# Values of all four recurrent heads in one projection of 512 columns, behind the gates of two heads

## The chip, the cores and the metric

The kernel runs on one core of one Trainium2 chip. The metric is the device time of one execution in microseconds, as the median of several runs. The engines named here are TensorE (PE; its weight loads are shown as PEld), VectorE (DVE), ScalarE (ACT), GpSimd (POOL) and SyncE (SP, which issues most DMAs). All products are made in float32 precision: an operand is split into a rounded high part and a remainder, and three matmuls (high by high, high by low, low by high) replace one.

## The reference, cut to what matters

Two blocks of two layers each run over 512 tokens of width 1024. The first block is an attention mixer, which the change leaves alone. Each layer of the second block has a recurrent mixer with eight heads of width 128 and then a gated FFN. The recurrent mixer is what the change touches:

```python
proj = h @ w_in                       # 512 x 1024 by 1024 x 4096
rq, rk, rv, rg, hq, hf, hi, hg = split(proj)      # 512 columns each: 4 heads of 128
r_out = retention_chunkwise(rotary(rq), rotary(rk) * 128 ** -0.5, rv, log_gamma)
q_h = silu(hq); k_in = (1 - lb) * sigmoid(-hf); log_f = log_sigmoid(hf) + log1p(lb * exp(-hf))
g_out = hgrn2_chunkwise(q_h, log_f, k_in, hi)
merged = concat(head_norm(r_out) * silu(rg), head_norm(g_out) * silu(hg))
x = x + g1 * (merged @ w_out)
```

The values are `hi` for the four HGRN2 heads and `rv` for the four retention heads. They are used as the right operand of the last product of a head, with the tokens on the partitions.

## The kernel before, in words

Activations lie with the 1024 features on the partitions, as eight pairs of tiles `hh`, `hl` (high part and remainder) of 128 x 512 tokens. A weight tile `wr` holds 128 x 1024 numbers (512 KB). One queue of weights serves the whole program: `next_w` gives the next one, starts the DMA of one some places ahead on SP's queue, and has ScalarE (L149) and VectorE (L150) split one into `wh` and `wl`. There are 2 buffers of `wr` and 3 of `wh` and `wl`. The array of host weights `w_in_2` is stored in the order in which `next_w` asks for it.

A gemm (`gemm`, `mm3`, L172 to L174) has a weight as stationary operand and 512 tokens as moving columns: 24 matmuls of 512 columns give one 128 x 512 tile `g` in PSUM with features on the partitions. Values are needed the other way round, with tokens on the partitions. `gemm_tok` (`tok_step`, L195 to L197) does that: the activations are stationary, 128 tokens at a time, and the weight is moving. A pair of heads has 256 value columns, so each matmul has 256 columns, and one PSUM tile `g` takes two blocks of tokens. `v_pair` makes the values of two heads: two weight tiles, two PSUM tiles, 96 matmuls, and two ScalarE copies (L1386) into the tile `v`, of which there are two buffers.

`ssm_layer` runs a layer. For each HGRN2 head it asks for the gate gemm (`hgrn_prep`: L1447 to L1458 give `k` and the cumulated logs `c`), the query gemm (`silu_ps`: three ScalarE steps L1463 to L1465, one VectorE step L1466), for every second head `v_pair`, and then the head itself (`hgrn`). A head is a chain of levels: VectorE and ScalarE make a tile `xl`, TensorE multiplies it with itself, and VectorE puts the result into the score tile `st`. The first level is L1532, then come L1537, L1546, six times L1558, and L1565; the product with the values is L1575. Normalising the output and turning it (`tail`, L1404) is left to the next head. The two gemms of head 0 are made in the stage before (`cross`), as `first`. After the HGRN2 heads follow four retention heads: two gemms with a rotation and a split each (`rotary`, `parts`, L217 and L218), for every second head `v_pair`, then score products, a decay mask (L1435) and the product with the values (L1440). Behind them come the eight output gates. In the first of the two layers VectorE also does background work, a matrix-vector product for the next modulation (L481).

The order on an engine is set by a scheduler when the program is built. Each engine then serves its own instructions in that order; where several are ready, the one that stands earlier in the program goes first. In the second block there are four PSUM buffers of tag `g`, four of tag `m` (products of the heads), 9 buffers of `u` (128 x 512 work tiles, also `k`, `c`, `q` of a head) and 3 of `xl`; a tile waits until a buffer of its tag is free.

The lines of `ssm_layer` that set the order are

```python
            q = silu_ps(oq)
            if h % 2 == 0:
                v = v_pair()
            tail = hgrn(l, h, k, c, q, [v[:, j, (h % 2) * P:(h % 2 + 1) * P] for j in range(4)], y[4 + h])
```

Of the kernel before, what the change touches and what calls it, by code (L numbers as in the profile page):

```python
# [20 lines left out]
P = 128  # L21
D = 1024
KT = 8
# [13 lines left out]
def tile_model(ctx: ExitStack, tc: tile.TileContext, a: dict, out: bass.AP, dbg=None):  # L37
# [1342 lines left out]

    def v_pair():
        os_ = [pt("g"), pt("g")]
        gemm_tok([(os_[0], hs2[0], 0), (os_[1], hs2[0], 2)])
        v = sb("v", [P, 4, 2 * P], F32, 2, sub[0])
        for i in range(2):
            act(v[:, 2 * i:2 * i + 2].rearrange("p a b -> p (a b)"), os_[i], AF.Copy)  # L1386
        return v
# [190 lines left out]
    def ssm_layer(l, hs, first):  # L1578
# [9 lines left out]
        tail = lambda: None  # L1588
        for h in range(HEADS):
            if h == 0:  # L1590
                (w, o), (w, oq) = first
            else:
                w = next_w()
                o = pt("g")
                gemm(o, w, hs)
            tail()
            k, c = hgrn_prep(l, h, o)
            if h > 0:
                w = next_w()
                oq = pt("g")  # L1600
                gemm(oq, w, hs)
            q = silu_ps(oq)
            if h % 2 == 0:
                v = v_pair()
            tail = hgrn(l, h, k, c, q, [v[:, j, (h % 2) * P:(h % 2 + 1) * P] for j in range(4)], y[4 + h])
        for h in range(HEADS):
            w = next_w()
            o = pt("g")
            gemm(o, w, hs)
            tail()  # L1610
            q = rotary(o, 1.0)
            q = (q, *parts(q))
            background(4)
            w = next_w()
            o = pt("g")
            gemm(o, w, hs)
            k = rotary(o, 128.0 ** -0.5)
            k = (k, *parts(k))
            if h % 2 == 0:
                v = v_pair()  # L1620
            tail = retention(h, q, k, [v[:, j, (h % 2) * P:(h % 2 + 1) * P] for j in range(4)], y[h])
        open_sub(f"mo{l}")
# [128 lines left out]
def _mixed(w, order):  # L1751
    w = np.asarray(w).reshape(KT, P, -1, P)
    r = []
    for t in order:
        if isinstance(t, tuple):
            b = w[:, :, list(t[:2])].reshape(2, 4, P, 2 * P).transpose(0, 2, 1, 3)
# [6 lines left out]
def _layout(i):  # L1763
# [22 lines left out]
    r["w_in_2"] = _f(np.stack([_mixed(g["w_in_2"][l], [  # L1786
        20, 16, (24, 25), 21, 17, 22, 18, (26, 27), 23, 19, 0, 4, (8, 9), 1, 5, 2, 6, (10, 11), 3, 7,
        12, 13, 14, 15, 28, 29, 30, 31]) for l in range(2)]))
# [77 lines left out]
```

## Time and profile before

| what | value |
|---|---|
| median of 3 runs | 2091.86 us (2086.92 to 2094.16) |
| time of the profiled execution | 2093.33 us |
| its span | 2091.5 us |
| TensorE busy | 2017.1 us, 96% of the span |
| TensorE weight loads busy | 1744.2 us, 83% |
| VectorE busy | 1416.8 us, 68% |
| ScalarE busy | 951.7 us, 46% |
| mean granted TensorE clock | 0.991 of full speed |

The span goes from the first to the last instruction of the profiled execution; its time is 1.8 us longer. Times below are in microseconds from the start of the span. A matmul is shown with its own duration, which overlaps that of the next one; the distance between two starts is what it costs in a stream. "x8" behind a row means that eight of the same kind were merged into it. A bracket at the end of a row gives the idle time of the engine before it and what ended it. The recurrent mixer of the first layer lies at about 766 to 998 us and that of the second at about 1436 to 1660 us.

### The profile page before, as it was taken

What the parts mean: (1) busy time and instruction counts of PE and PEld (TensorE: products, weight loads), DVE (VectorE), ACT (ScalarE), POOL (GpSimd) and SP (SyncE); (2) the same over time, 40 slices, a digit from 0 to 9 for tenths busy, and PEclk for the clock granted to TensorE, in tenths of its full rate; (3) what the DMA queues carried; (4) which work ended last, traced back from release to release, by engine and by line L of the source; (5) the groups of instructions that cost most, each with busy time, mean ns of one, the idle gap of its engine ahead of it and who ended that gap; (6) DMA issues with size and microseconds to landing.
All of it is one profiled execution on the core that took longest, in us unless ns stands there. A gap on an engine that the chain in (4) does not pass through costs nothing.

```text
span 2091.5 us, 30721 instructions
## 1 busy us (share of the span) xinstructions
PE 2017.1 (96%) x11642; PEld 1744.2 (83%) x11642; DVE 1416.8 (68%) x2733; ACT 951.7 (46%) x1655; POOL 204.0 (10%) x204
## 2 busy tenths in 40 slices
PE   5899999999999999999999999999999999999998
PEld 3798988899898889988888888888998888888887
DVE  6889998578667488888677775238876655444323
ACT  4536567343547456435453333226543544333322
POOL 5401011130101120000110000002000030000000
PEclk9999999999999999999999999999999999999999
DMA  7342224644011332255456664323122223232332
GB/s 266 100 134 85 93 92 132 213 138 133 31 61 51 121 125 81 84 169 184 146 159 215 217 209 144 101 83 101 60 71 72 90 73 108 94 101 92 92 103 76
DMA packets 96132, 245.97 MB, mean 118 GB/s; under 512 B 12592, under 2 KB 17952, under 8 KB 95728
## 3 DMA queue, kind: packets, MB, share of 16 engines
q1 hardware_dynamic: 94752, 242.90, 36.7%
q8 instruction: 92, 1.51, 0.3%
q0 software_dynamic: 656, 0.57, 0.1%
q10 hardware_dynamic: 576, 0.52, 0.1%
q14 instruction: 56, 0.46, 0.1%
HBM read 239.76 MB, written 4.19 MB: 117 GB/s over the span
## 4 chain that ended last, share of the span: by engine, by line
PE 79%; DVE 11%; ACT 3%; issue 2%; DMA 2%; POOL 1%; DVEq 0%; SPq 0%; POOLq 0%; ACTq 0%
PE g L173 19%; PE g L172 19%; PE g L174 19%; PE g L196 3%; PE g L197 3%; PE g L195 3%; PE m L1558 2%; PE m L947 2%; DVE gs L481 1%; DMA gr<-w_mod 1%; PE s L921 1%; DVE wl L150 1%; PE s L922 1%; PE m L940 1%; PE m L1575 1%
## 5 line engine op out<-in xcount | busy, mean ns | idle before, releaser
L173 PE MATMUL g<-hl,wh 128*128 128x512 f32 (+1 forms) x1320 | 508.2, 385 | 12.9 <-DVE hl L296 11.4
L174 PE MATMUL g<-hh,wl 128*128 128x512 f32 (+1 forms) x1320 | 504.9, 383 | 1.0 <-POOL wl L334 0.8
L172 PE MATMUL g<-hh,wh 128*128 128x512 f32 (+1 forms) x1320 | 505.2, 383 | 0.2 <-ACT wh L153 0.2
L150 DVE TENSOR_TENSOR wl<-wr,wh 128x1024 fp32r<-128x1024 f32 (+1 forms) x270 | 326.1, 1209 | 251.0 <-ACT wh L149 247.3
L149 ACT ACTIVATE wh<-wr 128x1024 fp32r<-128x1024 f32 (+1 forms) x270 | 281.9, 1044 | 411.6 <-PE g L173 369.1
L173 PEld LDWEIGHTS g<-hl,wh 128*128 128x128 f32 x1320 | 249.9, 189 | 62.2 <-DVE hl L296 17.7
L174 PEld LDWEIGHTS g<-hh,wl 128*128 128x128 f32 x1320 | 250.1, 189 | 45.5 <-POOL wl L334 1.1
L172 PEld LDWEIGHTS g<-hh,wh 128*128 128x128 f32 x1320 | 249.9, 189 | 44.2 <-ACT hh L292 0.7
L481 DVE SCALAR_TENSOR_TENSOR gs<-gr,cb 128x512 bf16<-128x512 f32 x304 | 209.9, 691 | 101.7 <-DMA gr<-ada_w 81.9
L197 PE MATMUL g<-wh,hl 128*128 128x256 f32 x704 | 202.3, 288 | 5.2 <-DVE hl L254 3.2
L196 PE MATMUL g<-wl,hh 128*128 128x256 f32 x704 | 203.8, 290 | 2.8 <-DVE wl L150 2.3
L195 PE MATMUL g<-wh,hh 128*128 128x256 f32 x704 | 203.5, 289 | 1.6 <-ACT hh L251 1.6
L235 POOL TENSOR_TENSOR acc<-acc,ta 128x512 f32<-128x512 f32 (+1 forms) x28 | 39.6, 1413 | 1249.9 <-ACT ta L230 1249.9
L172 PE MATMUL g<-g2h,wh 128*128 128x512 f32 (+1 forms) x396 | 145.1, 366 | 0.1
L174 PE MATMUL g<-g2h,wl 128*128 128x512 f32 (+1 forms) x396 | 144.9, 366 | 0.0
L173 PE MATMUL g<-g2l,wh 128*128 128x512 f32 (+1 forms) x396 | 144.7, 365 | 0.0
L197 PEld LDWEIGHTS g<-wh,hl 128*128 128x128 f32 x704 | 136.6, 194 | 7.0 <-DVE hl L254 4.0
L196 PEld LDWEIGHTS g<-wl,hh 128*128 128x128 f32 x704 | 136.7, 194 | 4.6 <-DVE wl L150 2.5
L195 PEld LDWEIGHTS g<-wh,hh 128*128 128x128 f32 x704 | 136.6, 194 | 2.6 <-ACT hh L251 1.9
L1675 ACT ACTIVATE t<-t,k_conv_b 128x512 f32<-128x512 f32 x44 | 31.8, 724 | 140.9 <-DVE t L1673 140.8
L172 PEld LDWEIGHTS g<-g2h,wh 128*128 128x128 f32 x396 | 74.7, 189 | 12.6 <-DVE y L1067 0.5
L173 PEld LDWEIGHTS g<-g2l,wh 128*128 128x128 f32 x396 | 74.7, 189 | 12.2
(416 smaller groups left out, 3755.8 us busy)
## 6 DMA issues: line engine op xcount, KB each, us to landing
wr<-w_in SPq DMA_DIRECT2D x112, 512.0 KB, 3.5
gr<-ada_w SPq DMA_DIRECT2D x192, 256.0 KB, 3.2
wr<-w_gate SPq DMA_DIRECT2D x44, 512.0 KB, 3.6
wr<-w_val SPq DMA_DIRECT2D x44, 512.0 KB, 3.5
gr<-w_mod SPq DMA_DIRECT2D x64, 256.0 KB, 2.9
wr<-w_out SPq DMA_DIRECT2D x32, 512.0 KB, 3.5
wr<-w_down SPq DMA_DIRECT2D x32, 512.0 KB, 3.5
raw<-w_mod_n SPq DMA_DIRECT2D x16, 512.0 KB, 6.8
```

The lines of the kernel that those rows point to most:

```text
L149: act(hi[:, :k], raw[:, :k], AF.Copy)
L150: V.tensor_tensor(out=lo[:, :k], in0=raw[:, :k], in1=r32(hi[:, :k]), op=ALU.subtract)
L172: PE.matmul(o, whi, xhi, start=start, stop=False)
L173: PE.matmul(o, whi, xlo, start=False, stop=False)
L174: PE.matmul(o, wlo, xhi, start=False, stop=stop)
L195: PE.matmul(ob, xh[:, sl], whi[:, k], start=fst, stop=False, skip_group_check=True)
L196: PE.matmul(ob, xh[:, sl], wlo[:, k], start=False, stop=False, skip_group_check=True)
L197: PE.matmul(ob, xl[:, sl], whi[:, k], start=False, stop=lst, skip_group_check=True)
L235: add()
L481: V.scalar_tensor_tensor(out=s, in0=t, scalar=1.0, in1=cb, op0=ALU.mult, op1=ALU.mult, accum_out=dst[:, i, m:m + 1])
L947: PE.matmul(o[:, qq * P:(qq + 1) * P], dt[:, j, qq * P:(qq + 1) * P], v, start=(j == 0), stop=(j == len(vs) - 1), skip_group_check=True)
L1558: PE.matmul(u[:, j * 64:(j + 1) * 64], x[:, j * P:(j + 1) * P], xq[:, j * nb:(j + 1) * nb], start=True, stop=True)
```

## The change

The values of all four heads are now made by one projection, `v_heads`. The four weight tiles of the values are stored so that each holds two of the eight k steps of all 512 value columns. `v_heads` takes four PSUM tiles `g`, one for each block of 128 tokens, and for each weight tile runs through the four blocks: activations stationary, 512 weight columns moving, 6 matmuls per block and weight tile. The tile `v` is 128 x 4 x 512 with one buffer, where there were two buffers of 128 x 4 x 256; four ScalarE copies fill it.

The order of the program changes with it. The gate and query gemms of a head are asked for one head ahead: those of heads 0 and 1 come first, then the values of all heads, then head 0; the gates of head 2 stand between head 0 and head 1, and so on. In the retention heads the values of all four come behind the query and key of head 0. The order of the weights in `w_in_2` follows.

```diff
@@ -1378,12 +1378,21 @@
     def u_():
         return sb("u", [P, T], F32, 9, sub[0])
 
-    def v_pair():
-        os_ = [pt("g"), pt("g")]
-        gemm_tok([(os_[0], hs2[0], 0), (os_[1], hs2[0], 2)])
-        v = sb("v", [P, 4, 2 * P], F32, 2, sub[0])
-        for i in range(2):
-            act(v[:, 2 * i:2 * i + 2].rearrange("p a b -> p (a b)"), os_[i], AF.Copy)
+    def v_heads():
+        os_ = [pt("g") for _ in range(4)]
+        hs = hs2[0]
+        for c in range(4):
+            whi, wlo = [t.rearrange("p a b -> p (a b)").rearrange("p (k n) -> p k n", n=T) for t in next_w()]
+            for b, o in enumerate(os_):
+                sl = slice(b * P, (b + 1) * P)
+                for k in range(2):
+                    xh, xl = hs[2 * c + k]
+                    PE.matmul(o, xh[:, sl], whi[:, k], start=c == k == 0, stop=False)
+                    PE.matmul(o, xh[:, sl], wlo[:, k], start=False, stop=False)
+                    PE.matmul(o, xl[:, sl], whi[:, k], start=False, stop=c == 3 and k == 1)
+        v = sb("v", [P, 4, T], F32, 1, sub[0])
+        for b, o in enumerate(os_):
+            act(v[:, b], o, AF.Copy)
         return v
 
     hs2 = [None]
@@ -1586,24 +1595,22 @@
         if l == 0:
             bg[0] = ada0
         tail = lambda: None
-        for h in range(HEADS):
+
+        def gate_steps(h):
             if h == 0:
                 (w, o), (w, oq) = first
             else:
                 w = next_w()
                 o = pt("g")
                 gemm(o, w, hs)
-            tail()
             k, c = hgrn_prep(l, h, o)
             if h > 0:
                 w = next_w()
                 oq = pt("g")
                 gemm(oq, w, hs)
-            q = silu_ps(oq)
-            if h % 2 == 0:
-                v = v_pair()
-            tail = hgrn(l, h, k, c, q, [v[:, j, (h % 2) * P:(h % 2 + 1) * P] for j in range(4)], y[4 + h])
-        for h in range(HEADS):
+            return k, c, silu_ps(oq)
+
+        def rot_steps(h, tail):
             w = next_w()
             o = pt("g")
             gemm(o, w, hs)
@@ -1615,10 +1622,21 @@
             o = pt("g")
             gemm(o, w, hs)
             k = rotary(o, 128.0 ** -0.5)
-            k = (k, *parts(k))
-            if h % 2 == 0:
-                v = v_pair()
-            tail = retention(h, q, k, [v[:, j, (h % 2) * P:(h % 2 + 1) * P] for j in range(4)], y[h])
+            return q, (k, *parts(k))
+
+        prev = gate_steps(0)
+        for h in range(HEADS):
+            nxt = gate_steps(h + 1) if h + 1 < HEADS else None
+            if h == 0:
+                v = v_heads()
+            tail()
+            tail = hgrn(l, h, *prev, [v[:, j, h * P:(h + 1) * P] for j in range(4)], y[4 + h])
+            prev = nxt
+        for h in range(HEADS):
+            q, k = rot_steps(h, tail)
+            if h == 0:
+                v = v_heads()
+            tail = retention(h, q, k, [v[:, j, h * P:(h + 1) * P] for j in range(4)], y[h])
         open_sub(f"mo{l}")
         ys = []
         for m in range(KT):
@@ -1752,7 +1770,10 @@
     w = np.asarray(w).reshape(KT, P, -1, P)
     r = []
     for t in order:
-        if isinstance(t, tuple):
+        if isinstance(t, list):
+            b = w[:, :, t].reshape(4, 2, P, 4 * P).transpose(0, 2, 1, 3)
+            r += [b[j].reshape(P, KT, P) for j in range(4)]
+        elif isinstance(t, tuple):
             b = w[:, :, list(t[:2])].reshape(2, 4, P, 2 * P).transpose(0, 2, 1, 3)
             r += [b[j].reshape(P, KT, P) for j in (t[2:] or (0, 1))]
         else:
@@ -1784,7 +1805,7 @@
     r["ada_w_2"] = _f(g["ada_w_2"].transpose(0, 2, 1).reshape(2, 48, P, D))
     r["ada_b_2"] = _f(np.stack([_cols(g["ada_b_2"][l]) for l in range(2)]))
     r["w_in_2"] = _f(np.stack([_mixed(g["w_in_2"][l], [
-        20, 16, (24, 25), 21, 17, 22, 18, (26, 27), 23, 19, 0, 4, (8, 9), 1, 5, 2, 6, (10, 11), 3, 7,
+        20, 16, 21, 17, [24, 25, 26, 27], 22, 18, 23, 19, 0, 4, [8, 9, 10, 11], 1, 5, 2, 6, 3, 7,
         12, 13, 14, 15, 28, 29, 30, 31]) for l in range(2)]))
     for n in ("w_out_2", "w_gate_2", "w_val_2", "w_down_2"):
         r[n] = _f(np.stack([_wtiles(g[n][l]) for l in range(2)]))
```

## Rows read from the trace of the kernel before

**Rows 1.** The page: busy time by engine, and the chain that ended last.

```profile
PE 2017.1 (96%) x11642; PEld 1744.2 (83%) x11642; DVE 1416.8 (68%) x2733; ACT 951.7 (46%) x1655; POOL 204.0 (10%) x204
...
PE 79%; DVE 11%; ACT 3%; issue 2%; DMA 2%; POOL 1%; DVEq 0%; SPq 0%; POOLq 0%; ACTq 0%
```

**Rows 2.** Stretches, each column one engine's busy time; then granted clock, DMA.

```profile
804.00:832.00 28.00, 28.00 (x214) 26.44 (x214) 25.36 (x65) 16.49 (x35) 0.00 (x0) 1.00 0.24 76
...
888.00:960.00 72.00, 70.72 (x414) 61.70 (x413) 60.09 (x123) 23.48 (x37) 0.00 (x0) 1.00 0.53 172
...
1474.00:1502.00 28.00, 28.00 (x216) 26.54 (x215) 24.96 (x61) 17.11 (x36) 0.00 (x0) 1.00 0.19 62
```

**Rows 3.** The tile v: ScalarE copies out of PSUM, ns least, median and most.

```profile
L1386 ACT ACTIVATE v<-g x16: 591/597/598, 773.2 to 1602.1; 128x512 f32<-128x512 f32 x16
```

**Rows 4.** Timeline of TensorE, head 2: start, duration, line, operation.

```profile
828.66 0.28 PE L196 MATMUL g<-wl,hh 128*128 128x256 f32 x1
...
832.36 0.28 PE L197 MATMUL g<-wh,hl 128*128 128x256 f32 x1
832.48 1.03 PE L1532 MATMUL m<-xl 128*128 128x256 f32 x4
```

**Rows 5.** Timeline of TensorE, a run of gemm matmuls in the recurrent stage.

```profile
1524.55 0.40 PE L174 MATMUL g<-hh,wl 128*128 128x512 f32 x1
...
1529.36 0.39 PE L174 MATMUL g<-hh,wl 128*128 128x512 f32 x1
```

**Rows 6.** Timeline of TensorE, a run of gemm matmuls in the FFN.

```profile
1101.80 0.39 PE L173 MATMUL g<-hl,wh 128*128 128x512 f32 x1
...
1105.88 0.39 PE L173 MATMUL g<-hl,wh 128*128 128x512 f32 x1
```

**Rows 7.** Lines of TensorE from 749 to 765.97: the crossing into the first layer.

```profile
L195 PE MATMUL g<-wh,hh 128*128 128x256 f32 x5 | 1.4, 281 | 0.0
```

**Rows 8.** Timeline of TensorE, the crossing into the second layer.

```profile
1429.52 0.58 PE L173 MATMUL g<-hl,wh 128*128 128x256 f32 x1 [1.63 <-DVE hl L296]
1429.90 0.41 PE L174 MATMUL g<-hh,wl 128*128 128x256 f32 x1
...
1432.25 0.41 PE L196 MATMUL g<-wl,hh 128*128 128x256 f32 x1
```

**Rows 9.** Timeline of VectorE, head 2: the second half of the first level.

```profile
829.37 0.42 DVE L1525 TENSOR_TENSOR xl<-u,u 128x256 f32<-128x256 f32 x1
```

**Rows 10.** Timeline of TensorE, first layer: values, first and last products of heads.

```profile
765.98 0.28 PE L196 MATMUL g<-wl,hh 128*128 128x256 f32 x1
...
776.69 1.13 PE L1532 MATMUL m<-xl 128*128 128x256 f32 x4 [0.37 <-DVE xl L1525]
...
792.74 0.68 PE L1565 MATMUL m<-xl 128*64 128x64 f32 x8
...
803.96 1.07 PE L1532 MATMUL m<-xl 128*128 128x256 f32 x4
...
874.86 0.68 PE L1565 MATMUL m<-xl 128*64 128x64 f32 x8
```

**Rows 11.** Lines, 765 to 905: busy, mean ns of one; the longest silu step.

```profile
L1464 ACT ACTIVATE u<-u,one_c 128x512 f32<-128x512 f32 x4 | 2.9, 718 | 0.0
```

**Rows 12.** Lines of TensorE from 776.69 to 874.86: gemm and value matmuls.

```profile
L173 PE MATMUL g<-hl,wh 128*128 128x512 f32 x64 | 25.9, 404 | 0.0
...
L195 PE MATMUL g<-wh,hh 128*128 128x256 f32 x36 | 10.4, 290 | 0.0
```

**Rows 13.** Lines of VectorE from 776 to 888: splits of weights, background work.

```profile
L150 DVE TENSOR_TENSOR wl<-wr,wh 128x1024 fp32r<-128x1024 f32 x12 | 14.4, 1216 | 0.4 <-ACT wh L149 0.3
...
L481 DVE SCALAR_TENSOR_TENSOR gs<-gr,cb 128x512 bf16<-128x512 f32 x10 | 6.8, 685 | 0.8 <-DMA gr<-ada_w 0.7
```

**Rows 14.** Timeline of TensorE, second retention head of the two layers.

```profile
910.71 0.50 PE L172 MATMUL m<-uh,uh 128*128 128x512 f32 x1 [0.64 <-ACT uh L217]
...
1579.91 0.50 PE L172 MATMUL m<-uh,uh 128*128 128x512 f32 x1 [0.28 <-ACT uh L217]
```

## The prediction

> **What bounds the kernel now.** I read the engine totals first, then the two recurrent stages by stretches of 28 us, then single instructions. TensorE is busy 96% of the span, and 79% of the chain that ended last is its own work [rows 1]. In the stretches of the recurrent heads it stands at 28.00 of 28.00 us in both layers, at the full granted clock, with VectorE right behind at 25.36 and 24.96 us; in the retention heads of the first layer TensorE is at 70.72 and VectorE at 60.09 of 72 us [rows 2]. So in the stage that the change touches, TensorE's own work sets the time, there is almost no idle time to win, and VectorE is near enough to become the bound if the order spoils its cover. Those are the two halves of the forecast: what TensorE saves, and whether the new order lets it starve.
>
> **What the new projection saves.** Before, each of the 8 calls of v_pair issues 96 matmuls of 256 columns: 768 in all. After, each of the 4 calls of v_heads issues 4 weight tiles x 4 token blocks x 2 x 3 = 96 matmuls of 512 columns: 384 in all. The columns streamed, the weight tiles, their loads and splits, and the 16 copies out of PSUM (0.597 us each, [rows 3]) stay as they are; only the cost of a matmul beside its columns can fall. "Busy" of one matmul overlaps its neighbours, so I take starts. From the second to the last 256-column matmul of one unbroken run are 31 steps in 3.70 us: 0.1194 us each [rows 4]. The 512-column matmuls in the busy stage take 21 steps in 4.81 us, 0.2290 us [rows 5]; in the quiet FFN stage 18 steps in 4.08 us, 0.2267 us [rows 6]. Old: 768 x 0.1194 = 91.7 us. New: 384 x 0.2290 = 87.9, or x 0.2267 = 87.1 us. The saving is 3.8 to 4.6 us; I take 4.2, for the blocks run partly beside busy and partly beside quiet engines. Nothing here is large: two narrow steps are 0.2388 us against one wide step of 0.229.
>
> The Trainium skill, "TensorE: Matmul & The Clock Gate", section "Back-to-back issue gap", speaks against even that: it puts the isolated gap at columns / 2.4 GHz plus 2.5 ns, which would be 109.2 and 215.8 ns, and an estimate from the two is 768 x 109.2 - 384 x 215.8 ns, a saving of only 1.0 us. The rows differ [rows 4 to 6]: beyond the columns at 2.4 GHz they show 13 to 16 ns a matmul, in a stream where each has its own weights.
>
> **What moves at the start of a layer.** Until now v_pair was the next work after the crossing from the stage before, and 13 of its recorded matmuls (5, 4 and 4 on its three lines, the first of them in [rows 7]) ran inside the crossing, while that waited for the second half of the norm; the other layer shows the same counts. Now the gate of head 1 is next, with 512 columns over both halves. Its steps go by k, and those whose k is normalised can fill the same holes. Bounds: nothing lost, or all 13 x 0.12 x 2 layers = 3.1 us lost. I take nothing, because a hole opens while the crossing waits for a later k, when the earlier ones are there. What such a hole can cost beyond itself is seen in layer 1: after 1.63 us of idle time, 256-column matmuls start 0.214 us apart (1429.90 to 1432.25, 11 steps in 2.35 us) instead of 0.119, which is the lower clock level, 1.2 GHz [rows 8]; 14 matmuls at it cost 1.3 us. No DMA moves against another: the weights are loaded in the order in which they are used, before and after.
>
> **The block of 33 us.** The order of issue follows the order of the program where several things are ready. The row to see is head 2: its first tile xl is done at 829.79 [rows 9], yet TensorE runs values until 832.36 and starts L1532 only at 832.48 [rows 4]. So in the new order hgrn(0) will wait behind the gate of head 1 (48 x 0.229 = 11.0 us) and all values (96 x 0.229 = 22.0 us). The crossing ends at 765.98 and L1532 of head 0 starts at 776.69 [rows 10]; it goes to about 766.0 + 33.0 - 1.5 = 797.5 (the 1.5 us are the 13 matmuls' worth in the crossing), some 21 us later. Queued behind it: VectorE can make x256, x128, the first level and the product kq, and then the three buffers of xl are full; it stands for about 10 us, except for splits of weights and the prep of head 1. The block has its own possible wait: it takes all four g buffers, and the last of them is free only when silu of head 1 is done. Block 3 asks for it 18 matmuls, 4.1 us, after the gate ends; three ScalarE steps of at most 0.72 us [rows 11] and a VectorE step of the same width are some 2.8 us. So no stall is costed; if one of those steps is queued late, it is 1 to 2 us per layer.
>
> Does VectorE's lost time come back as a stall of TensorE? From the first L1532 to the last L1565 of the four heads the old trace has 776.69 to 874.86, 98.2 us [rows 10]. In it ran 191 gemm matmuls and 108 value matmuls (lines of 64, 64 and 63, and three of 36, [rows 12]), 43.7 + 12.9 us, and 0.4 us idle; the heads' own matmuls are the other 41.2 us, 10.3 per head. In the new order the cover that is left from 797.5 is: gates of heads 2 and 3, 22.0; q and k of the first retention head, 11.0; the retention values, 22.0. With the heads' own 41.2 that is 96.2 us of work for TensorE before it must wait for head 3. The chain of a head, from L1532 to L1565, is 16.05 us [rows 10]. So TensorE starves only if heads follow each other more slowly than (96.2 - 16.05) / 3 = 26.7 us. They now follow at 27.3 us (776.69 to 803.96), but with TensorE full; VectorE's work in 28 us is 25.4 [rows 2], and part of it is background gemv and splits that may move into its 10 idle microseconds. With 23 to 25.4 us a head (25.4 less, at the lower end, the background of 10 x 0.685 us over four heads and part of a split of 1.2 us, [rows 13]), the chain is 85 to 92 us, below 96.2. So L1565 of head 3 comes at 882 to 890, 8 to 15 us later than now, but TensorE has work until 893.7 and the loss is zero; the values of retention are the reserve. Bounds: nothing, or what the first rival gives.
>
> The retention values have one more wait: v has one buffer of all heads, so their copies wait until hgrn(3) has used the old one. With the chain above, the projection still has some 4 to 11 us to run then, and nothing is lost.
>
> **Retention heads without values.** Heads 1 and 3 now wait for uh once each: 0.64 us in layer 0 and 0.28 us in layer 1 [rows 14]. Heads 0 and 2 have values in front and show none. After the change heads 1, 2 and 3 are without. One wait more per layer: 0.64 + 0.28 = 0.9 us. Bounds: nothing, or twice that, 1.8, since the lag of heads in a row may add up.
>
> **Sum.** 2093.33 (the profiled execution: span 2091.5 and 1.8 around it) - 4.2 + 0.9 = 2090.0 us. The median of the three runs lies 1.5 us below that execution, so the forecast for the median is 2091.86 - 3.3 = 2088.6 us. That is 0.16% less, below the 0.3% (6.3 us) that a measurement of this kernel can tell from no change.
>
> **Rivals.**
> A, slower: VectorE becomes the bound of the recurrent heads. One mechanism: the block holds hgrn(0) back by 21 us, and heads keep following at 28 us or more, because VectorE and ScalarE are served in program order and only 3 of the 9 u buffers are free beside k, c, q of two heads. Then the chain is 16 + 3 x 28 = 100 us against 96.2 of cover: TensorE idles 4 us per layer, and each such idle time brings the lower clock for 1.3 us more. 2 x 5.3 = 10.6 us against the saving of 3.3: 2099 us. It decides from 26.7 us a head on; it is a slower result by over 6.3 us only from about 28. For it: VectorE is at 91% already. Against it: prep of the next head is out of the way, and the old gaps of 11.2 us between L1565 and the next L1532 (792.74 to 803.96, [rows 10]) hold gemm work that VectorE need not wait for now.
>
> B, the change saves nothing: the first block loses its fill in the crossing (3.1 us), or a wide matmul with a full tile as moving operand costs as much as two narrow ones, 0.2388. With the first the forecast becomes 2091.7, with the second 2091.86 + 0.9 = 2092.8: 2092 us, no change. By the page's gap it would be 2091.86 - 1.0 + 0.9, the same. For it: no row shows a 512-column weight tile as moving operand. Against it: three families of 512-column matmuls lie at 0.227 to 0.229.
>
> C, faster: the best price, 4.6 us, and the waits of retention (0.64 + 0.28, twice each) and of the first L1532 (0.37 us idle in layer 0) vanish, since the longer stock of gemm work covers them: 4.6 + 1.8 + 0.4 = 6.8 us, 2085.1 us, just outside 0.3%.
>
> **Chances and range.** Forecast 0.55, A 0.19, B 0.13, C 0.13. The forecast and B are within 0.3%; of C and of the forecast's edge I count 0.14 as faster; A and a little of B's edge make 0.20 slower; 0.66 remain. The predicted time is 2088.6. The range runs from C with the runs' scatter, 2084, up to A at 2099, leaving out 1 in 10 above (A with more than 4 us idle) and 1 in 10 below. Within the forecast alone it is 2085.5 to 2091.5: the bounds 3.8 to 4.6, 0 to 1.8, and 1 to 2 us of a late silu or a spread of runs.
>
> **What the new profile would show.** Right: a group of 384 matmuls of 512 columns on the lines of v_heads, starts 0.227 to 0.231 us apart, and TensorE at 28 of 28 us in the recurrent stretches; L1532 of head 0 about 21 us later in the stage, L1565 of head 3 some 8 to 15 us later; VectorE idle near 10 us beside the first value block; three waits for uh per layer. Wrong: TensorE idle over 2 us before a value copy or an L1558; a granted clock under 1.00 in the recurrent stage; copies of retention values waiting for L1575; or a pitch of 0.239, which makes the saving nothing.

## The result, and the profile after

The changed kernel takes 2115.79 us (median of 5 runs, 2106.9 to 2117.83), the kernel before 2094.16 us beside it: a ratio of 1.0100, 95% interval 1.0071 to 1.0128. It is slower, by some 21 us, and lies outside the range of the prediction.

The totals of the page come first, as in [rows 1]:

```profile
PE 2028.9 (96%) x11258; PEld 1735.0 (82%) x11258; DVE 1418.0 (67%) x2733; ACT 951.3 (45%) x1655; POOL 204.8 (10%) x204
```

There are 384 matmuls fewer, as planned, and yet TensorE is busy 11.8 us longer. Fewer matmuls with more busy time means matmuls that ran longer: the mean granted clock fell from 0.991 to 0.982. Where, the stretches say. The columns are as in [rows 2]: busy time and count of TensorE, its weight loads, VectorE, ScalarE and GpSimd, then granted clock, DMA share and GB/s.

```profile
825.00:853.00 28.00, 27.81 (x179) 24.39 (x179) 24.82 (x55) 16.59 (x38) 0.00 (x0) 1.00 0.14 46
872.00:893.00 21.00, 17.17 (x91) 15.36 (x90) 16.20 (x35) 7.36 (x19) 0.00 (x0) 0.67 0.00 1
1553.00:1576.00 23.00, 20.66 (x102) 18.02 (x101) 18.11 (x42) 8.47 (x23) 0.00 (x0) 0.68 0.06 21
...
1016.00:1023.00 7.00, 6.68 (x18) 5.25 (x18) 3.85 (x9) 4.63 (x8) 0.00 (x0) 0.56 0.42 143
```

Heads 1 and 2 run full and at full clock, like the heads before. Three stretches don't: head 3 of HGRN in each layer (872 and 1553), and seven microseconds in the output projection of layer 0 (1016). VectorE isn't full in them either, and in head 3 of layer 0 the DMA is still (0.00, 1 GB/s), so no weight was being fetched.

To say what each costs, I took the starts of TensorE's last matmul of four kinds and made stretches between them: R0, from the last projection of the attention block to the last product of scores and values of retention in layer 0; P0, from there to the last matmul on a y2l, the last but one of the output projection of layer 0; R1, from the last matmul of layer 0's FFN to the last such product in layer 1; all, from the last projection of the attention block to the last matmul of the program's last FFN. What lies ahead of R0 is the same in all kernels and differed by -3 to +4 us from one profiled execution to another, so it is left out here. In microseconds, one profiled execution each:

```
                                    R0      P0      R1      all
before                          216.86   83.15  214.79  1337.23
after                           224.98   88.84  222.67  1358.63
12 u buffers                    226.89   86.09  222.28  1357.56
wide values, old order          223.68   86.24  214.42  1348.70
new order, narrow pairs         220.17   83.02  214.21  1339.86
g 5, m 3                        215.29   87.79  213.65  1339.09
only HGRN values wide           219.94   83.67  216.01  1343.37
q, k of head 0 early, u 12      219.34   87.32  214.75  1343.55
g 5, m 3, four steps moved      215.73   83.83  213.60  1335.51
before, g 5, m 3                218.25   82.95  214.75  1336.33
eight steps moved               226.17   84.72  221.05  1354.02
g 5, m 3, eight steps moved     225.05   83.59  212.14  1342.56
the same, q, k early, u 12      218.87   84.35  213.64  1339.83
narrow pairs, g 5, m 3          221.46   84.03  214.70  1344.61
```

After minus before is 8.1 in R0, 5.7 in P0, 7.9 in R1, and 21.4 in all: these three places are the whole difference.

**Head 3.** The timeline of TensorE in layer 0, start and duration, idle time and its cause in brackets:

```profile
872.46 1.03 PE L1541 MATMUL m<-xl 128*128 128x256 f32 x4
...
874.89 0.39 PE L1392 MATMUL g<-wh,hl 128*128 128x512 f32 x1
875.12 1.00 PE L1567 MATMUL m<-xl,u 128*128 128x64 f32 x8
877.19 1.10 PE L1567 MATMUL m<-xl 128*128 128x64 f32 x8 [1.07 <-DVE xl L1533]
879.78 3.65 PE L1567 MATMUL m<-xl 128*128 128x64 f32 x16 [1.49 <-DVE xl L1534]
884.71 3.65 PE L1567 MATMUL m<-xl 128*128 128x64 f32 x16 [1.27 <-DVE xl L1534]
888.11 0.77 PE L1390 MATMUL g<-wh,hh 128*128 128x512 f32 x1
...
890.39 0.63 PE L1392 MATMUL g<-wh,hl 128*128 128x512 f32 x1
890.95 1.12 PE L1574 MATMUL m<-xl 128*64 128x64 f32 x8
```

L1390 to L1392 are the wide values, L1541, L1567 and L1574 the first, middle and last products of a head (L1532, L1558 and L1565 before). From 875 to 888 TensorE has nothing but head 3, and waits for VectorE between its levels. The three waits are 3.83 us; the clock falls with them. Two slices show when:

```profile
878.00:879.00 1.00, 0.29 (x3) 0.16 (x2) 1.00 (x3) 0.77 (x3) 0.00 (x0) 0.88 0.00 0
...
892.00:893.00 1.00, 1.00 (x7) 0.96 (x7) 0.94 (x3) 0.38 (x1) 0.00 (x0) 0.79 0.00 0
```

The grant is 1.00 before the first, 0.50 between the two and 1.00 after the second, so TensorE ran at the lower level from about 878.8 to 892.4, 13.7 us. The first wait was over by then; some 1.0 us of the second and the whole third, 2.3 us, lie inside. The other 11.4 us lost half of themselves, 5.7 us. Together with the waits 9.5 us: the lower clock costs more than the waits that bring it. In layer 1 two such waits are enough:

```profile
1561.31 3.59 PE L1567 MATMUL m<-xl 128*128 128x64 f32 x16 [1.07 <-DVE xl L1533]
1566.17 3.64 PE L1567 MATMUL m<-xl 128*128 128x64 f32 x16 [1.28 <-DVE xl L1534]
```

There the grant is 0.93 from 1561.0 to 1561.5 and 0.50 right after, so only the first wait lay before the fall.

So TensorE ran out of other work. How much was there? Its lines from 797.7 to 891.7, from the first L1541 to the last L1574, in the columns of [rows 12]:

```profile
L172 PE MATMUL g<-hh,wh 128*128 128x512 f32 x48 | 19.6, 408 | 0.0
...
L1392 PE MATMUL g<-wh,hl 128*128 128x512 f32 x15 | 6.3, 423 | 0.0
L1390 PE MATMUL g<-wh,hh 128*128 128x512 f32 x14 | 6.3, 449 | 0.0
L1391 PE MATMUL g<-wl,hh 128*128 128x512 f32 x14 | 6.2, 443 | 0.0
```

All gemms of the gates and of q and k ran (48 x 3 = 144). Of the 43 wide ones the first, at 797.54, still belongs to the HGRN values, so only 42 of the 96 retention values ran; 54 x 0.229 = 12.4 us of work lay there unused. Before the stall it was 36: two blocks of tokens, three weight tiles, six matmuls each. VectorE's splits of weights (L150) pause from 865.27 to 897.70, which fits the three buffers of wh and wl; a fourth buffer of these was not tried. The values fill four PSUM buffers g. In the order of the trace only two of the four blocks were open, and the other two buffers were held by q and k of retention head 0, whose gemms end at 859.6. What frees those buffers is a ScalarE copy each, L1419:

```profile
877.76 0.42 ACT L1527 ACTIVATE u<-u 128x256 f32<-128x256 f32 x1 [2.71 <-DVE u L1526]
881.00 0.42 ACT L1527 ACTIVATE u<-u 128x256 f32<-128x256 f32 x1 [1.57 <-DVE u L1526]
883.50 0.58 ACT L1419 ACTIVATE u<-g 128x512 f32<-128x512 f32 x1
...
885.92 0.58 ACT L1419 ACTIVATE u<-g 128x512 f32<-128x512 f32 x1
```

They come 24 and 26 us after the gemms. In the nine microseconds ahead of them ScalarE was idle for 2.71 and 1.57 us, waiting for head 3: the copies stand behind steps of head 3 in its order.

**Output projection of layer 0.** TensorE's timeline shows one long wait and a row of slow matmuls:

```profile
1016.32 0.79 PE L172 MATMUL g<-y2h,wh 128*128 128x512 f32 x1 [4.04 <-ACT y2h L217]
1016.91 0.63 PE L173 MATMUL g<-y2l,wh 128*128 128x512 f32 x1
...
1021.60 0.63 PE L173 MATMUL g<-y2l,wh 128*128 128x512 f32 x1
```

Before, the same wait was there with 0.26 us, a sign that there was nothing to spare:

```profile
1003.46 0.73 PE L172 MATMUL g<-y2h,wh 128*128 128x512 f32 x2 [0.26 <-ACT y2h L217]
```

What y2h waits for is the gate product of VectorE, L1650:

```profile
1015.64 0.63 ACT L217 ACTIVATE y2h<-tg 128x512 fp32r<-128x512 f32 x1 [2.95 <-DVE tg L1650]
```

In front of that on VectorE stand background products, L481, whose data come by DMA. Their group from the last product of retention to the last y2h, before (960 to 1003.5):

```profile
L481 DVE SCALAR_TENSOR_TENSOR gs<-gr,cb 128x512 bf16<-128x512 f32 x19 | 13.0, 686 | 2.2 <-DMA gr<-ada_w 2.1
```

and after (969.6 to 1016.3):

```profile
L481 DVE SCALAR_TENSOR_TENSOR gs<-gr,cb 128x512 bf16<-128x512 f32 x21 | 14.4, 688 | 6.5 <-DMA gr<-ada_w 6.4
```

Two products more, and 6.4 us of waiting for their data instead of 2.1, in the same queue as the gates. Why the data came later no run here separates. Layer 1 has no background work, and its output projection took 82.6 us before and after.

### The profile page after: what moved, and what is told of

Read it like the earlier page. It is cut to its first block, busy times and chain, and to the rows that moved or that the text cites. A ratio compares the mean times of both kernels' runs of the same rounds, so it can differ in the third digit from the quotient of the medians.

```text
span 2114.7 us, 29959 instructions
## 1 busy us (share of the span) xinstructions
PE 2028.9 (96%) x11258; PEld 1735.0 (82%) x11258; DVE 1418.0 (67%) x2733; ACT 951.3 (45%) x1655; POOL 204.8 (10%) x204
## 5 line engine op out<-in xcount | busy, mean ns | idle before, releaser
L173 PE MATMUL g<-hl,wh 128*128 128x512 f32 (+1 forms) x1320 | 507.1, 384 | 13.7 <-DVE hl L296 12.3
L150 DVE TENSOR_TENSOR wl<-wr,wh 128x1024 fp32r<-128x1024 f32 (+1 forms) x270 | 326.0, 1208 | 254.0 <-ACT wh L149 249.8
L481 DVE SCALAR_TENSOR_TENSOR gs<-gr,cb 128x512 bf16<-128x512 f32 x304 | 209.8, 690 | 111.0 <-DMA gr<-ada_w 91.2
L197 PE MATMUL g<-wh,hl 128*128 128x256 f32 x448 | 130.0, 290 | 5.5 <-DVE hl L254 3.2
L196 PE MATMUL g<-wl,hh 128*128 128x256 f32 x448 | 130.7, 292 | 2.3 <-DVE wl L150 2.3
L195 PE MATMUL g<-wh,hh 128*128 128x256 f32 x448 | 130.6, 292 | 1.8 <-ACT hh L251 1.7
L197 PEld LDWEIGHTS g<-wh,hl 128*128 128x128 f32 x448 | 87.8, 196 | 7.6 <-DVE hl L254 4.0
L196 PEld LDWEIGHTS g<-wl,hh 128*128 128x128 f32 x448 | 87.7, 196 | 3.3 <-DVE wl L150 2.5
L195 PEld LDWEIGHTS g<-wh,hh 128*128 128x128 f32 x448 | 87.8, 196 | 2.9 <-ACT hh L251 2.0
L172 PEld LDWEIGHTS g<-g2h,wh 128*128 128x128 f32 x396 | 74.7, 189 | 12.9 <-DVE y L1067 0.5
```

Of the source, the lines that this page charges most:

```text
L150: V.tensor_tensor(out=lo[:, :k], in0=raw[:, :k], in1=r32(hi[:, :k]), op=ALU.subtract)
L172: PE.matmul(o, whi, xhi, start=start, stop=False)
L173: PE.matmul(o, whi, xlo, start=False, stop=False)
L195: PE.matmul(ob, xh[:, sl], whi[:, k], start=fst, stop=False, skip_group_check=True)
L196: PE.matmul(ob, xh[:, sl], wlo[:, k], start=False, stop=False, skip_group_check=True)
L197: PE.matmul(ob, xl[:, sl], whi[:, k], start=False, stop=lst, skip_group_check=True)
```

## The experiments

Theory S, and G as its sharper form: the wide retention values want four g buffers at once; q and k of retention head 0 hold two, so the reserve for head 3 is less than half of what the prediction counted. S took the copies that free them to be late for want of u buffers; G says that they are late by ScalarE's order. Rival B (not the B of the prediction; V in the first expectations): the block of all values in front delays the heads, whatever the reserve. W, in two of them, says that the wide projection itself is what costs. Theory O is for the output projection: it waits because of the background products. Each run is timed against runs of the kernel before on the same chip.

**1. More u buffers.**

```diff
-        return sb("u", [P, T], F32, 9, sub[0])
+        return sb("u", [P, T], F32, 12, sub[0])
```

> The changed kernel with 12 buffers of u in place of 9. Theory S (stock): in head 3 TensorE runs out of work, because q and k of the first retention head keep two of the four g buffers until a u buffer is free for their copy, so that only 36 of the 96 retention value matmuls can run. Then three more u buffers free g early, all 96 can run, the idle time in head 3 (about 7 us with the lower clock, in each layer) is gone, and the ratio to the kernel before is 0.997 to 1.004. Rival V: VectorE and ScalarE are late after the first block of values, and that alone sets the end of the stage; more buffers change nothing and the ratio stays at 1.010.

Measured: 2112.42 us, ratio 1.0102 (1.0080 to 1.0124). R0 and R1 do not fall (R0 is 1.9 us longer, R1 0.4 shorter), and the copies are hardly earlier, at 881.73 and 884.20:

```profile
881.73 0.58 ACT L1419 ACTIVATE u<-g 128x512 f32<-128x512 f32 x1
884.20 0.58 ACT L1419 ACTIVATE u<-g 128x512 f32<-128x512 f32 x1
```

The shortage is not one of u: this part of S falls.

**2. Only the width: wide values in the old order** (for each recurrent part behind the gates of its first head).

```diff
+            if h == 0:
+                v = v_heads()
-            if h % 2 == 0:
-                v = v_pair()
```

> The kernel before with its own order of gates, but all four heads' values in one wide projection, at head 0 of each kind. S: k, c, q of one head only hold u buffers, so q and k of retention are copied out at once and all 96 value matmuls can run; the ratio is 0.996 to 1.002, with the saving of some 4 us. Rival W: the wide projection itself is what costs (four PSUM tiles at once, one buffer of v); the ratio stays near 1.010. V: the block in front of head 0 is 22 us and not 33 us, so about two thirds of the loss stays, 1.006.

Measured: 2104.27 us, ratio 1.0043 (1.0019 to 1.0067). R1 is as before, R0 is 6.8 longer, P0 3.1. W's 1.010 is excluded; V's 1.006 and the edge of S's range lie in the interval, but S's reason did not come: it had all 96 retention values run beside the heads, and 18 did in layer 0 and 32 in layer 1. Wide values lose in layer 0 without the new order too. There the clock was 0.83 from 862 to 884, the end of the heads.

**3. Only the order: narrow pairs, both asked for where the wide values stand.**

```diff
-                v = v_heads()
+                vs = [v_pair(), v_pair()]
```

> The new order (gates of two heads, then all values, gates a head ahead), but the values as two narrow pairs back to back, each with two PSUM tiles and 96 matmuls of 256 columns. S: a pair needs only the two g buffers that are left, so the whole first pair (11.5 us in place of 8.3) runs in head 3 and is copied into a free v buffer, and then the second; TensorE has work, and the ratio is 0.999 to 1.004. V: the block in front of head 0 is as long as in the change, and the ratio stays at 1.010. W: with the narrow pairs the loss is gone, 1.000.

Measured: 2100.29 us, ratio 1.0044 (1.0027 to 1.0061). In the profiled execution R0 is 3.3 longer and P0 and R1 are as before; 3.7 us of that execution's excess lie ahead of the recurrent stage, so by the stretches the order alone cost some 3 us, less than by the runs. A narrow pair needs two g buffers, and in these two layers TensorE doesn't starve at head 3. By the runs the two costs, 0.43% for the width and 0.44% for the order, nearly add up to the 1.00% of the change, whose interval they don't leave. That the two together do more than each alone is shown by layer 1: R1 is not longer with either, and 7.9 us longer with both. What the order costs in layer 0 was not separated further.

**4. One g buffer more**, at the cost of a buffer of the heads' products.

```diff
-        PSB.update(g=4, m=4)
+        PSB.update(g=5, m=3)
```

> The changed kernel with five g buffers and three m buffers in place of four and four. S: three blocks of the retention values can run over three weight tiles, 54 matmuls in place of 36, some 4 us more of stock in each layer; the ratio falls to about 1.005, unless three m buffers hold the heads up. V and W: 1.010 or more.

Measured: 2094.71 us, ratio 1.0010 (1.0000 to 1.0019). TensorE's value lines from 795.5 to 885.5, as above:

```profile
L1391 PE MATMUL g<-wl,hh 128*128 128x512 f32 x21 | 8.5, 407 | 0.0
L1392 PE MATMUL g<-wh,hl 128*128 128x512 f32 x21 | 8.3, 397 | 0.0
L1390 PE MATMUL g<-wh,hh 128*128 128x512 f32 x20 | 8.3, 414 | 0.0
```

The stretches of head 3 in the two layers, in the columns of the first table of stretches:

```profile
868.00:888.00 20.00, 19.47 (x129) 16.78 (x128) 17.94 (x41) 9.14 (x23) 0.00 (x0) 1.00 0.06 23
1541.00:1561.00 20.00, 19.93 (x129) 17.16 (x128) 18.19 (x42) 9.88 (x26) 0.00 (x0) 1.00 0.08 29
```

Two of the 62 are the end of the HGRN values, so it is 60 values instead of 42: 18 x 0.229 = 4.1 us more reserve. The clock stayed at 1.00, and R0 fell by 9.7 and R1 by 9.0 us, over twice the added work; the ratio is well below the 1.005 expected. P0 stays 4.6 us above before: the output projection is another matter.

**5. The retention values alone undone**: HGRN wide, retention in two narrow pairs back to back.

```diff
+                v = sb("v", [P, 4, T], F32, 1, sub[0])
+                v_pair(v, 0)
+                v_pair(v, 1)
-                v = v_heads()
             tail = retention(h, q, k, [v[:, j, h * P:(h + 1) * P] for j in range(4)], y[h])
```

> HGRN values wide, retention values again in two narrow pairs (asked for back to back). Theory G (the wide retention block wants four g buffers at once, two of which the gemms of q and k of head 0 hold, so that only 36 of its 96 matmuls are a reserve): a narrow pair needs two buffers, so some 14.8 us of values (124 of 192 matmuls, as in the run with narrow pairs) cover head 3 and the starving of head 3 goes in both layers: about 2099 us, ratio 1.003 to 1.005. Rival B (the block of all heads in front delays the heads, whatever the reserve behind): 2110 us, ratio 1.009.

Measured: 2093.51 us, ratio 1.0016 (1.0005 to 1.0027). R0 fell by 5.0, P0 by 5.2, R1 by 6.7 us. The block in front of the heads is the same as in the changed kernel, so rival B falls as the main cause. The starving shrinks but is not gone: TensorE stands at 18.82 of 20 us from 868 to 888, at a clock of 0.91. In layer 0 108 of the 192 narrow values, some 12.9 us at the 0.1194 of [rows 4], ran beside the heads.

**6. The copies moved forward**: with 12 u buffers, q and k of retention head 0 and their rotation asked for ahead of head 3.

```diff
             tail()
+            if h == HEADS - 1:
+                rot0 = rot_steps(0, lambda: None)
             tail = hgrn(l, h, *prev, [v[:, j, h * P:(h + 1) * P] for j in range(4)], y[4 + h])
```

> The changed kernel with 12 u buffers, q and k of retention head 0 and their rotary steps asked for ahead of head 3 of HGRN. Theory G: the copies that free the two g buffers stand ahead of head 3's work on ScalarE, so all four blocks of the retention values can run beside head 3 (54 more matmuls, 12.4 us): 12.4 us less starving than in the run with 12 u buffers alone at most, 2099 to 2104 us, ratio 1.004 to 1.006. Rival B: rotary work on VectorE ahead of head 3 makes it later, and nothing is won: 2112 us or more, ratio 1.010 or more.

Measured: 2094.88 us, ratio 1.0020 (1.0009 to 1.0031), 17 us below the run with 12 u buffers alone. ScalarE's copies in layer 0:

```profile
856.17 0.58 ACT L1419 ACTIVATE u<-g 128x512 f32<-128x512 f32 x1
858.18 0.60 ACT L1419 ACTIVATE u<-g 128x512 f32<-128x512 f32 x1 [0.96 <-PE g L174]
```

TensorE's value lines from 795.4 to 891.9:

```profile
L1392 PE MATMUL g<-wh,hl 128*128 128x512 f32 x32 | 12.9, 402 | 0.0
L1391 PE MATMUL g<-wl,hh 128*128 128x512 f32 x32 | 12.6, 393 | 0.0
L1390 PE MATMUL g<-wh,hh 128*128 128x512 f32 x31 | 12.2, 403 | 0.0
```

The stretches of head 3 in the two layers:

```profile
871.00:894.00 23.00, 23.00 (x143) 19.96 (x141) 21.18 (x50) 8.92 (x22) 0.00 (x0) 1.00 0.27 89
1547.00:1570.00 23.00, 23.00 (x144) 19.95 (x143) 19.74 (x43) 9.69 (x23) 0.00 (x0) 1.00 0.18 54
```

The copies are 26 us earlier than in experiment 1, 93 of the 96 values run beside the heads (two of the 95 are the end of the HGRN values), and TensorE stands at 23.00 of 23.00 us at full clock in both layers. No buffer g was added and no work taken away, and the 12 u buffers alone had given nothing: the order of the program, which puts ScalarE's copies behind head 3, was what kept the two g buffers. The edit also moves TensorE's and VectorE's part of q and k, and it was not run with 9 u buffers. This is the sharpest case for G, and the gain is more than the expected 8 to 13 us.

**7. Background work moved** from the gates to the HGRN values, four of the 32 steps of layer 0 with g 5 and m 3.

```diff
                 v = v_heads()
+                background(4)
...
             g = silu_ps(o, "tg")
-            background(2)
+            background(2 - m % 2)
```

> The changed kernel with five g and three m buffers, and four of the 32 background steps of layer 0 asked for at the HGRN values instead of in the output projection. Theory O (the wait of 3.25 us for the last y2h of layer 0, and the half clock behind it, come from the background's products in front of the gates on VectorE): it goes, 4 us below the run with five and three alone: about 2090.5 us, ratio 0.999. Rival: the background is not what the gates wait for, or it delays the heads as much: 2094 to 2096 us, ratio 1.001 to 1.002.

Measured: 2089.27 us beside 2090.29 for the kernel before, ratio 0.9985 (0.9973 to 0.9997). P0 fell by 4.0 us against experiment 4, R0 and R1 stayed. The wait for y2h is only 0.6 us shorter, 2.65 instead of 3.25 us, but the clock stays up behind it. TensorE's timeline, with 512-column matmuls 0.23 us apart soon after the wait:

```profile
1001.11 0.50 PE L172 MATMUL g<-y2h,wh 128*128 128x512 f32 x1 [2.65 <-ACT y2h L217]
...
1002.86 0.39 PE L174 MATMUL g<-y2h,wl 128*128 128x512 f32 x1
1003.09 0.39 PE L172 MATMUL g<-y2h,wh 128*128 128x512 f32 x1
```

This is the one version faster than both kernels; by the ratio it is 0.15%, by the medians 1.0 us, and the interval nearly reaches 1. The kernel before with background steps moved was not run.

**8. Control: the kernel before with g 5 and m 3.**

```diff
-        PSB.update(g=4, m=4)
+        PSB.update(g=5, m=3)
```

> The kernel before with five g and three m buffers, as a control. Theory G (the fifth g buffer mends a shortage that the wide projection made): no gain, 2091 to 2093 us, ratio 1.000. Rival D (five and three is better for any order): 2085 us, ratio 0.997; with three m buffers too few for its heads: 2096 us, ratio 1.002.

Measured: 2091.88 us, ratio 1.0004 (0.9994 to 1.0013). The fifth g buffer gives the old kernel nothing: it mends what the change had made scarce.

**9. Background alone**: eight steps moved, one instead of two at each gate, four and four buffers.

```diff
                 v = v_heads()
+                background(8)
...
             g = silu_ps(o, "tg")
-            background(2)
+            background(1)
```

> The changed kernel with eight of layer 0's 32 background steps asked for at the HGRN values, and one at each gate of the output projection instead of two. Theory O (the wait for the last y2h in layer 0 comes from the background's products ahead of the gates on VectorE and goes with half of them): 4 to 6.9 us less than the changed kernel, the starving of head 3 stays in both layers: ratio 1.007 to 1.008. Rival: the gates are late because the heads were, background or not: ratio 1.010.

Measured: 2110.33 us, ratio 1.0088 (1.0066 to 1.0109). The interval holds both expectations. The stretches part them: P0 fell by 4.1 of the 5.7 us, R0 and R1 kept their starving. The products between retention and the last y2h:

```profile
L481 DVE SCALAR_TENSOR_TENSOR gs<-gr,cb 128x512 bf16<-128x512 f32 x13 | 9.0, 691 | 2.9 <-DMA gr<-ada_w 2.6
```

13 instead of 21, and 2.6 us of waiting for data. So O holds for most of P0; TensorE still waited 2.24 us for y2h, and no run here explains that rest.

**10 and 11. The edits of 4 and 9 together, without and with the early q and k of 6.**

```diff
-        PSB.update(g=4, m=4)
+        PSB.update(g=5, m=3)
...
+                background(8)
...
-            background(2)
+            background(1)
```

> The same with five g and three m buffers. With four steps moved the wait for the last y2h was still 2.81 us; with eight it goes if theory O holds: some 2 to 3 us below that run, ratio 0.997. Rival: no further gain, 0.9985.

> The same with 12 u buffers and q and k of retention head 0 ahead of head 3. Theory G says that the fifth buffer and the early copies mend the same shortage: no more than 0 to 2 us below the run without the early copies, ratio 0.996 to 0.998. Rival B: the rotary work delays head 3, ratio 0.999.

Measured: 2094.86 us, ratio 1.0016 (1.0006 to 1.0027), and 2095.57 us, ratio 1.0013 (1.0002 to 1.0024). Both missed: slower than with four steps moved. In the first, P0 and R1 are good (83.59 and 212.14, the shortest R1 of all), but R0 is 9.3 us longer than with four steps. The profiled execution took 2100.32 us, the longest of its twelve, so its rows say more of that execution than of the median. TensorE waits at other places there:

```profile
896.86 0.66 PE L1413 MATMUL m<-c_ident,t 128*128 128x128 f32 x4 [2.25 <-DVE t L1407]
927.97 0.50 PE L172 MATMUL m<-uh,uh 128*128 128x512 f32 x1 [1.82 <-ACT uh L217]
```

The norm of HGRN head 3 and a split of retention came late, and the clock was 0.93 from 888 to 912. Why the scheduler's order puts them there with eight steps and not with four stays open.

**12. What the width saves when nothing starves**: the new order with narrow pairs, g 5 and m 3.

```diff
-        PSB.update(g=4, m=4)
+        PSB.update(g=5, m=3)
...
-                v = v_heads()
+                vs = [v_pair(), v_pair()]
```

> The new order with narrow pairs, five g and three m buffers: beside the wide kernel with five and three (1.001) this shows what 512 columns save. By the durations of the trace of before 3.8 to 4.6 us: ratio 1.003. Rival (the saving is lost again even with five and three): 1.001 or less.

Measured: 2098.51 us, ratio 1.0040 (1.0024 to 1.0056), against 1.0010 (1.0000 to 1.0019) for the wide values with the same buffers. The difference is 0.3%, 6 us, with an uncertainty of some 4 us. That agrees with the 3.8 to 4.6 us of the durations, but does not prove them: the two profiled executions differ by 6.2 us in R0 and by only 1.1 us in R1, and in R0 the narrow kernel has a wait that is no price of a matmul, with a clock of 0.83 from 922 to 932:

```profile
922.73 0.50 PE L172 MATMUL m<-uh,uh 128*128 128x512 f32 x1 [2.24 <-ACT uh L217]
```

## Why the prediction was wrong, point by point

**The price of a matmul was right.** From 782.12 to 797.54 the new values take 68 steps in 15.42 us, 0.2268 us each, the quiet one of the two prices of [rows 5, 6]. TensorE's timeline:

```profile
782.12 0.39 PE L1390 MATMUL g<-wh,hh 128*128 128x512 f32 x1
...
797.54 0.39 PE L1392 MATMUL g<-wh,hl 128*128 128x512 f32 x1
797.77 0.59 PE L1541 MATMUL m<-xl 128*128 128x256 f32 x2
```

96 x (2 x 0.1194 - 0.2268) = 1.15 us for this block, 4.6 us if all four ran so, the upper end of 3.8 to 4.6. Experiment 12 agrees with it.

**The start of the layer was right.** The first L1541 was foreseen at 797.5 and came at 797.77. Nothing large was lost in the crossing.

**The heads were about right.** They follow one another at 27.5, 23.7 and 23.5 us (L1541 at 797.77, 825.25, 848.99 and 872.46), 24.9 on average, foreseen 23 to 25.4, and the last L1574 of head 3 starts at 891.7, after the stall, foreseen 882 to 890. Rival A's condition, 28 us a head, did not come; its outcome, TensorE idle at head 3 and then the lower clock, came all the same, with some 9.5 us a layer where it had 5.3.

**The step that failed is the cover: "the retention values, 22.0" in the sum of 96.2 us.** What could run of them was 42 matmuls, 42 x 0.229 = 9.6 us, so the cover was 83.8 us, and 6 of the 42 ran only in the stall itself. The prediction had asked about the four g buffers for the first block, where the last comes free some 2.8 us after its gemm, and not for the second, where two are held for 24 us. With 83.8 us of cover, TensorE starves from (83.8 - 16.05) / 3 = 22.6 us a head; every distance was above that. The loss was forecast as 0. If the rest of the sum held (per layer 2.1 saved, 0.6 or 0.3 us of uh waits), it was 8.1 + 2.1 - 0.6 = 9.6 us in layer 0 and 7.9 + 2.1 - 0.3 = 9.7 in layer 1; in layer 0 the waits and the lower clock of head 3 account for some 9.5 of it. Experiments 4, 5 and 6 lengthen this one cover in three ways, and each takes away most of the growth of R0 and R1.

**A step was missing: the background work of layer 0.** The prediction named L481 only inside the heads. Taking two blocks of values out of the retention heads made them shorter: from the first to the last product of scores and values 59.9 us instead of 69.6, the intended effect of moving the values forward. But VectorE had done 26 background products there, and did 20 now. Six more had run ahead of the first head (11 instead of 5), and two more stood ahead of the last y2h (21 instead of 19); four that had come behind it before came ahead now. So the gates, which had 0.26 us to spare, met two more products and 4.3 us more of waiting for data. In every kernel with the new order or wide values the wait for y2h grew, and much of what it cost was decided by the clock behind it: waits of 1.38 and 1.49 us (narrow pairs), 2.33 (only HGRN wide) and 2.65 us (four steps moved) left it at the full level, with P0 at 83.0 to 84.0; waits of 2.90, 2.99, 3.25, 3.30 and 4.04 us (wide retention values) brought the lower one, with P0 at 86 to 89. The length of the wait alone does not decide it: with eight steps moved (experiments 9 to 11), waits of 2.06, 2.24 and 2.49 us brought the lower level too, with P0 at 83.6 to 84.7.

**Waits for uh were right.** Three in layer 0, as foreseen for heads 1 to 3, where there had been two, the first of them in [rows 14]. TensorE's timeline:

```profile
929.99 0.50 PE L172 MATMUL m<-uh,uh 128*128 128x512 f32 x1 [0.64 <-ACT uh L217]
...
946.54 0.50 PE L172 MATMUL m<-uh,uh 128*128 128x512 f32 x1 [0.70 <-ACT uh L217]
...
964.26 0.50 PE L172 MATMUL m<-uh,uh 128*128 128x512 f32 x1 [0.55 <-ACT uh L217]
```

**The one buffer of v cost nothing**, as foreseen, though for another reason: the values were so late, their last matmul at 907.1, that head 3 had long done with the old ones.

With the cover mended and four steps moved the kernel is at 0.9985 of before, 3 us less, near what the prediction had for the change itself. That agrees with the price and does not prove the sum; the agreement is in part luck: this kernel has another split of the buffers and another place of the background work, and the new order cost 0.4% with narrow values (experiments 3 and 12), which the sum did not have. The prediction had taken the buffers for granted.

## What to carry to other kernels

Work counts as a reserve only if it can begin: for each piece, name the PSUM buffer it writes, who holds that now, and which instruction of which engine's order frees it. A wider tile that needs all buffers of its kind at once is only as ready as the last of them, and idle microseconds of TensorE can cost more than themselves through the clock behind them (here 3.8 us of waiting and 5.7 us of clock). And work that is moved out of a stage takes its cover away from whatever ran beside it: here two more background products, and longer waits for their data, stood in front of gates that had 0.26 us to spare.

## What the runs showed of the hardware

At the lower clock level the price changes in kind. From 1016.91 to 1021.60 wide matmuls start 0.426 us apart (11 steps in 4.69 us), and [rows 8] has 0.214 us for 256 columns: just the columns at 1.2 GHz, so there two narrow ones cost no more than a wide one. At 2.4 GHz 0.2268 and 0.1194 us are each 13 ns over the columns, and one of these 13 ns in two is all that the wide form saves. The Trainium skill, "TensorE: Matmul & The Clock Gate", section "Back-to-back issue gap", has, for the isolated gap, columns / 1.2 GHz at the low level, with which the trace agrees (an estimate from it is 426.7 ns for 512), and columns / 2.4 GHz plus 2.5 ns at the high one, by the same estimate 215.8 ns, where the trace shows 226.8.

The lower clock came with small gaps between short matmuls of head 3: in layer 1 it came right behind one idle time of 1.07 us, in layer 0 behind one of 1.07 us and the first half microsecond of the next, and it was back at the higher level only 13.7 us later. In experiment 4, with 4.1 us more of work in between, it stayed at 1.00.
